# The MLP's down products: banks of shared products summed in DRAM, and two pairs of K tiles as seven products

## The chip, the cores and the metric

The kernel runs on one core of one Trainium2 chip. The metric is the device time in microseconds of one execution; lower is better. Every time below is of the same program and inputs.

## The reference

Two layers of a decoder trunk on 256 tokens of width 2048: an attention mixer (a different one in each layer), an MLP, and a gated per-layer embedding. The part that matters here is the MLP, once in each layer:

```python
hn = rmsnorm(h, mlp_norm_g[i])
h = h + jnp.square(jax.nn.relu(hn @ mlp_w1[i])) @ mlp_w2[i]     # 2048 -> 8192 -> 2048
```

All values are float32.

## The kernel before

**Precision.** TensorE works on `fp32r` values. Each operand is split into a high part and the rest (`whi`, `wlo` for weights), and a product of two tiles is three matmuls of 128x128 by 128x512 (`terms`): high by high, low by high, high by low. So the third matmul of a product is the first that reads `wlo`.

**The stream of weights.** All weights come in one long list of parts. `Program.run` walks it: for the part at position `at` it issues loads up to seven parts ahead (SyncE's queue, five `raw` buffers), the high cast up to four ahead (ScalarE, L249, six `whi` buffers), the low subtraction up to three ahead (VectorE, L257, five `wlo` buffers), then lets the helpers that are under way (generators, one step for each part) issue their next instructions, then issues the part's matmuls. All instructions of an engine run in the order in which they were issued; there is no scheduler behind that. A helper's `yield` thus means "after one more part". An operation that waits holds up all that is queued behind it on its engine.

**Seven products in place of eight.** A plain part multiplies two K tiles by both halves of the tokens: four products, 12 matmuls. Two parts (two output columns of 512) make eight products. `pair_major` makes the eight of a *mixed* pair of K tiles from seven (Strassen's scheme in Winograd's form). A mixed pair c takes four items: `a` (two products, 6 matmuls), `b` (one, 3 matmuls), `t` and `u` (two each). The weights of `t` and `u` are not loaded but made by VectorE: `make_t` (L537) from a and b, `make_u` (L542, L543) from a, b and t, in place in b's `raw` buffer. The input forms come as tile `hf` (in the downs) or `xf` (in the ups). The products end in the two pairs of PSUM banks `c_banks` (tile `at`) and in four shared banks `P1`, `R6`, `Q5`, `Q7` (tile `mm`), which `seven_sums` (L807 to L812: one ScalarE copy, four VectorE operations) turns into the parts that are added to the two outputs' banks.

**The MLP.** The 8192 hidden columns are four blocks b of 2048, each of four quarters q of 512. `ups` and `up_mixed` make a block's hidden values: a bank's result goes through ReLU with the norm factor (L828), a square (L765), a transposition on VectorE (L706), a bounce through DRAM on POOL's DMA queue (L203 out, four loads L207 in), and is split into tile `h` (cast L774, subtraction L776). The number of steps between the landing and the cast is in `REST`, by block and quarter. For one quarter `up` goes on and makes the forms `hf` of a mixed pair: four small subtractions (L784 to L787), a cast (L791), a subtraction (L793).

`down_mixed(b, q)` multiplies a block's hidden values by W2 for two output quarters q and q+1; one pair of eight, `MIXED_DOWN = 1`, is mixed. It ends with the bank added to the sums (L892) and `keep_sum`, which stores the first block's result to a DRAM tile `y[q]` and adds the later ones to it with an accumulating transfer (L849, POOL). In the last block the sums are fetched, added, turned and added to x. Quarters 2 and 3 of the last block are plain `downs`.

The order of a layer's MLP is `ups(0,0)` and `ups(0,1)`, `up_mixed(0,2)`, then for each block `down_mixed(b,0)`, `up_mixed(b+1,0)`, `down_mixed(b,2)`, `up_mixed(b+1,2)`, and at the end `down_mixed(3,0)` and the two plain downs. A down is named (b,q) below. Rows of [P, 2, 512] for all these come from `row_tile`, four buffers.

Of the kernel before, what the change touches and what calls it, by code (L numbers as in the profile page):

```python
# [28 lines left out]
NFB = 4  # L29
# [5 lines left out]
DMA_AHEAD = 7  # L35
SPLIT_AHEAD = 3
RAW_BUFS, HI_BUFS, LO_BUFS = 5, 6, 5
MIXED_DOWN = 1
MIXED = (2, 3, 5, 6)
REST = ((6, 8, 2, 3), (4, 4, 2, 3))  # L40

G_ATTN, G_MLP, G_PLE, G_KV, G_FIN = 0, 2, 4, 6, 7

# [6 lines left out]
def f32(ap):  # L50
    return ap.bitcast(F32)
# [116 lines left out]
def kernel(ctx: ExitStack, tc: tile.TileContext, a: dict, out: bass.AP):  # L168
    nc = tc.nc
# [525 lines left out]
    def turned(src, new, eng=nc.sync):  # L695

        z = new("z")  # L700
        z5 = z.rearrange("p (b i j r) -> p j i b r", b=4, i=4, j=2)
        if isinstance(src, (list, tuple)):
            for j in range(2):
                nc.vector.transpose(z5[:, j], src[j].rearrange("p (i b s) -> p i b s", b=4, s=32))
        else:
            nc.vector.transpose(z5, src.rearrange("p j (i b s) -> p j i b s", b=4, s=32))  # L706
        yield
        w = new("w").rearrange("p (a n) -> p a n", a=4)
        g = bounce(z, "dU", w, eng)
        next(g)  # L710
        yield
        yield
        next(g, None)
        yield
        yield
        return w
# [18 lines left out]
    def mlp(layer, xg, norm, to, norm2, opening):  # L735
# [4 lines left out]


        y = [dpool.tile([P, D // 2], F32, tag=f"y{q}", name=f"y{q}", bufs=1) for q in range(4)]
        hid = [[None] * 16 for _ in range(NFB)]
        forms = [None] * (KT // 2)
        sums_so_far = {}
        turned_forms = [[None] * (KT // 2) for _ in range(NFB)]
# [4 lines left out]
        def row():  # L751
            return row_tile()
# [9 lines left out]
        def up(b, q, t, late=0):  # L762
            rest = REST[b > 0][q]

            nc.scalar.activation(t, t, AF.Square)  # L765
            for _ in range(2 + late):
                yield
            w = yield from turned(t, second if b == 0 and q == 1 else other if q % 2 else new, nc.gpsimd)
            for _ in range(rest):
                yield  # L770
            w4 = w.rearrange("p a (i j r) -> p a (i j) r", j=2, r=32)
            h = cur["z"].tile([P, 2, 4, T], F32R, tag="h", name="h", bufs=4)
            h5 = h.rearrange("p c i (j a r) -> p c a (i j) r", j=2, r=32)
            nc.scalar.copy(h5[:, 0], w4)  # L774
            yield
            nc.vector.tensor_sub(h5[:, 1], w4, f32(h5[:, 0]))  # L776
            for i in range(4):
                hid[b][4 * q + i] = (h[:, 0, i], h[:, 1, i])
            if q != MIXED_DOWN // 2:
                return  # L780

            n = MIXED_DOWN % 2 * 4
            a11, a21, a12, a22 = (w4[:, :, n + i] for i in range(4))
            nc.vector.tensor_sub(a22, a21, a22)  # L784
            nc.vector.tensor_sub(a21, a11, a21)
            nc.vector.tensor_sub(a11, a11, a22)
            nc.vector.tensor_sub(a12, a12, a11)  # L787
            yield
            f = cur["z"].tile([P, 2, 2 * T], F32R, tag="hf", name="hf", bufs=1)
            f5 = f.rearrange("p c (i a r) -> p c a i r", i=4, r=32)  # L790
            nc.scalar.copy(f5[:, 0], w4[:, :, n:n + 4])  # L791
            yield
            nc.vector.tensor_sub(f5[:, 1], w4[:, :, n:n + 4], f32(f5[:, 0]))  # L793
            turned_forms[b][MIXED_DOWN] = f

        def up_plain(b, q, ps0, ps1, mm):

# [46 lines left out]
            sums_so_far[q] = row()  # L844
            nc.gpsimd.dma_start(flat(sums_so_far[q]), y[q])

        def keep_sum(b, q, t):

            nc.gpsimd.dma_start(y[q], flat(t), **({"accum_op": ALU.add} if b else {}))  # L849

        def down(b, q, ps0, ps1, mm):
            t = row() if b < NFB - 1 else sums_so_far[q]
            for j, ps in enumerate((ps0, ps1)):
                if b < NFB - 1:
                    nc.scalar.copy(t[:, j], ps)
                else:
                    nc.vector.tensor_add(t[:, j], ps, t[:, j])
            yield
            if b < NFB - 1:
                keep_sum(b, q, t)  # L860
                return
            w = yield from turned(t, second if q == 1 else new)
            add_turned(q, w)
            yield
            yield from in_pairs(normed, q)
# [10 lines left out]
        def all_forms(these):  # L876
            for c in these:
                yield from x_forms(2 * c, G_MLP + layer, forms)
                yield
        taken_late(lambda: ups(0, 0, {4: [lambda: norm.factor(rows=True)]}), lambda: ups(0, 1), opening,  # L880
                   [lambda: all_forms(MIXED[:3])])
        def down_mixed(b, q):
            ts = []

            def sums(aux):
                yield from seven_sums(aux, ts)

            def done(i, ps):
                while not ts:
                    yield  # L890
                t = ts[i]
                nc.vector.tensor_add(t, ps, t)  # L892
                yield
                if b < NFB - 1:
                    keep_sum(b, q + i, t)
                    return
# [6 lines left out]
                yield from in_pairs(normed, q + i)  # L903

            m = MIXED_DOWN
            p = [c for c in range(KT // 2) if c != m]
            order = [(0, c) for c in p[:3]]
            order += [(m,)] + [(1, c) for c in p[:3]] if b else [(1, c) for c in p[:3]] + [(m,)]
            for n in (3, 5):
                order += [(i, c) for i in range(2) for c in p[n:n + 2]]  # L910
            pair_major(lambda i, c: a["w2"][layer * 128 + (b * 4 + q + i) * 8 + c], order, hid[b], turned_forms[b],
                       sums, done, {13: [lambda: all_forms(MIXED[3:])]} if (b, q) == (0, 0) else None, (3, 1, 0, 2))

        up_mixed(0, 2)
        for b in range(NFB):
# [13 lines left out]
    def flat(t):  # L929
        return t.rearrange("p j c -> p (j c)")  # L930
# [968 lines left out]
def _layout(i):  # L1899
    a = dict(_tables())  # L1900
# [12 lines left out]
    a["w_oA"] = _quads(i["a_w_out"][0])  # L1913
    a["w1"] = np.concatenate([_mixed(_quads(i["mlp_w1"][l]), range(2, 16, 2), mixed) for l in range(2)])
    a["w2"] = np.concatenate([_mixed(np.concatenate([_quads(i["mlp_w2"][l, b * D:(b + 1) * D]) for b in range(NFB)]),
                                     range(0, 14, 2), lambda b, q: (MIXED_DOWN,)) for l in range(2)])
# [35 lines left out]
```

## Time and profile before

| | us |
|---|---|
| median of 3 runs | 2421.25 (2420.17 to 2422.47) |
| profiled execution, its own time | 2421.02 |
| span of its profile | 2419.1 |

| engine | busy us | share |
|---|---|---|
| TensorE | 2409.0 | 100% |
| VectorE | 1988.5 | 82% |
| ScalarE | 1420.2 | 59% |
| GpSimd | 122.0 | 5% |

Matmuls are pipelined, and their records overlap: a matmul of 128x512 has 389 ns, but one starts every 227 ns. "PE" is TensorE, "PEld" its weight loads, "DVE" VectorE, "ACT" ScalarE, "POOL" GpSimd, "SP" SyncE; a name such as L257 is a line of the kernel. In a row of a timeline stand the start, the time, the engine, line and operation, output and inputs, and in brackets the idle time before it and what ended that. Where a row ends in x3, three neighbours of one kind are merged.

### The profile page before, as it was taken

To read this page: it belongs to the slowest core of one execution; us is meant where nothing else is said; L and a number is where in the kernel's file an instruction comes from. 1 tells how busy PE (TensorE), PEld (TensorE's weight loads), DVE (VectorE), ACT (ScalarE), POOL (GpSimd) and SP (SyncE) were. 2 spreads that over 40 slices of the span, in tenths; PEclk is the share of its full clock that TensorE was granted. 3 is DMA by queue.
4 is the path that set the end of the run, shared out by engine and by line. 5 is a ranking of instruction groups with operands and counts; after the bars stand their busy time and mean duration, and the time that the engine had idled before them with its cause. 6 is when DMAs were issued, how large, how long until landed. Compare 5 with 4: busy or idle time off the path is not lost.

```text
span 2419.1 us, 33339 instructions
## 1 busy us (share of the span) xinstructions
PE 2409.0 (100%) x11643; PEld 2029.3 (84%) x11643; DVE 1988.5 (82%) x2944; ACT 1420.2 (59%) x2069; POOL 122.0 (5%) x214
## 2 busy tenths in 40 slices
PE   9999999999999999999999999999999999999998
PEld 8888888888888888888888889988888888888887
DVE  7867687688898898896777989867899898889776
ACT  6544444566555655564564788756655565556456
POOL 0000000000001000100000000000100100100000
PEclk9999999999999999999999999999999999999999
DMA  8667666777778777879786854477867877777974
GB/s 284 200 220 213 199 206 196 220 222 247 231 244 242 255 211 241 244 253 283 251 245 204 262 173 121 129 235 210 251 231 234 246 254 220 242 252 224 297 240 148
DMA packets 167271, 549.05 MB, mean 227 GB/s; under 512 B 20096, under 2 KB 35904, under 8 KB 167104
## 3 DMA queue, kind: packets, MB, share of 16 engines
q1 hardware_dynamic: 150672, 494.73, 63.7%
q0 software_dynamic: 15856, 51.41, 8.5%
q8 instruction: 91, 1.49, 0.3%
q10 hardware_dynamic: 576, 0.79, 0.1%
q14 instruction: 76, 0.62, 0.1%
HBM read 500.20 MB, written 46.66 MB: 226 GB/s over the span
## 4 chain that ended last, share of the span: by engine, by line
PE 98%; DMA 1%; DVE 0%; ACT 0%; issue 0%; ACTq 0%; DVEq 0%
PE at L499 40%; PE at L595 14%; PE mm L595 13%; PE mm L390 11%; PE mm L499 7%; PE mm L392 6%; PE at L390 1%; DMA raw<-in_w 1%; PE at L392 1%; PE at L1774 1%; PE mm L1798 0%; PE mm L1537 0%; PE mm L1538 0%; PE mm L1004 0%; PE mm L1006 0%; PE mm L1005 0%
## 5 line engine op out<-in xcount | busy, mean ns | idle before, releaser
L257 DVE TENSOR_TENSOR wlo<-raw,whi 128x1024 fp32r<-128x1024 f32 (+1 forms) x943 | 1090.6, 1176 | 247.3 <-ACT whi L249 63.9
L249 ACT CAST whi<-raw 128x1024 fp32r<-128x1024 f32 (+1 forms) x943 | 932.8, 1017 | 471.9 <-PE mm L595 101.8
L499 PE MATMUL at<-whi,h 128*128 128x512 f32 x1624 | 500.6, 389 | 0.4 <-DVE h L776 0.4
L390 PE MATMUL mm<-xa,whi 128*128 128x512 f32 x1104 | 372.4, 396 | 0.0
L499 PEld LDWEIGHTS at<-whi,h 128*128 128x128 f32 x1624 | 304.9, 188 | 64.6 <-DVE h L776 1.3
L499 PE MATMUL at<-whi,xa 128*128 128x512 f32 x1144 | 352.3, 389 | 0.0
L499 PE MATMUL at<-wlo,h 128*128 128x512 f32 x812 | 315.9, 389 | 0.0
L392 PE MATMUL mm<-xa,wlo 128*128 128x256 f32 x1104 | 274.2, 278 | 0.0
L499 PEld LDWEIGHTS at<-whi,xa 128*128 128x128 f32 x1144 | 214.7, 188 | 44.6
L499 PE MATMUL at<-wlo,xa 128*128 128x512 f32 x572 | 222.5, 389 | 0.0
L392 PEld LDWEIGHTS mm<-xa,wlo 128*128 128x128 f32 x1104 | 207.4, 188 | 17.6
L390 PEld LDWEIGHTS mm<-xa,whi 128*128 128x128 f32 x1104 | 193.5, 188 | 31.0 <-issue 0.4
L595 PE MATMUL at<-whi,xa 128*128 128x512 f32 x672 | 208.4, 392 | 0.0
L595 PE MATMUL mm<-whi,xa 128*128 128x512 f32 x656 | 202.7, 390 | 0.0
L499 PEld LDWEIGHTS at<-wlo,h 128*128 128x128 f32 x812 | 152.4, 188 | 31.5
L249 ACT CAST whi<-ts 128x1024 fp32r<-128x1024 f32 x68 | 71.5, 1051 | 156.8 <-DVE ts L537 106.9
L595 PEld LDWEIGHTS at<-whi,xa 128*128 128x128 f32 x672 | 125.2, 189 | 26.0 <-issue 0.6
L595 PEld LDWEIGHTS mm<-whi,xa 128*128 128x128 f32 x656 | 122.5, 188 | 25.0
L595 PE MATMUL at<-wlo,xa 128*128 128x512 f32 x336 | 130.8, 390 | 0.0
L595 PE MATMUL mm<-wlo,xa 128*128 128x512 f32 x328 | 127.7, 389 | 0.0
L499 PEld LDWEIGHTS at<-wlo,xa 128*128 128x128 f32 x572 | 107.4, 188 | 22.3
L499 PE MATMUL mm<-whi,xf 128*128 128x512 f32 x324 | 99.8, 389 | 0.0
(433 smaller groups left out, 3222.2 us busy)
## 6 DMA issues: line engine op xcount, KB each, us to landing
raw<-in_w SPq DMA_DIRECT2D x512, 512.0 KB, 4.8
raw<-in_w_qk SPq DMA_DIRECT2D x96, 512.0 KB, 4.1
raw<-in_w_gate SPq DMA_DIRECT2D x64, 512.0 KB, 4.5
raw<-in_w_kv SPq DMA_DIRECT2D x48, 512.0 KB, 4.4
raw<-in_w_v SPq DMA_DIRECT2D x47, 512.0 KB, 4.5
y<-y POOLq DMA_DIRECT2D x32, 512.0 KB, 5.5
raw<-in_w_q SPq DMA_DIRECT2D x32, 512.0 KB, 4.2
raw<-in_w_oB SPq DMA_DIRECT2D x32, 512.0 KB, 4.2
```

The source lines that it names most:

```text
L249: nc.scalar.copy(hi[:, c], t[:, c])
L257: nc.vector.tensor_sub(lo[:, c], t[:, c], f32(hi)[:, c])
L390: nc.tensor.matmul(ps, hi[:, col:col + P], rhs, start=first, stop=False)
L392: nc.tensor.matmul(ps[:, :T], lo[:, col:col + P], rhs[:, :T], start=False, stop=last)
L499: nc.tensor.matmul(ps, x_, w_, start=b not in touched, stop=end and last[b] == n and i == 2)
L595: nc.tensor.matmul(st[j], *parts[j][i], start=k == i == 0, stop=k == kt - 1 and i == 2)
L1774: nc.tensor.transpose(tr[:, i * P:(i + 1) * P], src, ident)
```

## The change

1. **Two mixed pairs in each `down_mixed`**: `MIXED_DOWN = (1, 0)`. Both come from quarter 0 of the block's hidden values, so `up` makes both `hf` tiles there (two buffers in place of one), and W2 is laid out accordingly.
2. **The order of items.** From block 1 on: two plain items for output quarter q, the first mixed pair, two plain items for q+1, the second mixed pair, then eight plain items. In block 0: four plain items, both mixed pairs one after the other, then eight plain items. Before, there were three plain items, the pair, three plain items and eight more (in block 0: six, the pair, eight).
3. **Sums of the shared banks.** In blocks 0 to 2 the four shared banks are copied by ScalarE into two rows, and these are stored or added to two more DRAM tiles for each pair of output quarters (`shared`). The outputs' own banks are copied by ScalarE and stored or added as they are. The two L892 additions and the four VectorE sums of these downs go.
4. **`flush`** makes the sums once for each pair of output quarters: it loads the two rows, makes the four VectorE operations after five steps, and adds the two results to `y`. For quarters 0 and 1 it starts after the first item of `down_mixed(2,2)`, for 2 and 3 after the first of `down_mixed(3,0)`. The last block's down (`down_last`) is summed as before.
5. `REST` for quarter 0 of blocks 1 to 3 is 8 in place of 4.

```diff
-MIXED_DOWN = 1
+MIXED_DOWN = (1, 0)
-REST = ((6, 8, 2, 3), (4, 4, 2, 3))
+REST = ((6, 8, 2, 3), (8, 4, 2, 3))
...
+        shared = {q: [dpool.tile([P, D // 2], F32, tag=f"s{q}{i}", name=f"s{q}{i}", bufs=1) for i in range(2)] for q in (0, 2)}
...
-            if q != MIXED_DOWN // 2:
+            if q:
                 return
-            n = MIXED_DOWN % 2 * 4
-            a11, a21, a12, a22 = (w4[:, :, n + i] for i in range(4))
-            ...
+            fs = {}
+            for c in MIXED_DOWN:
+                a11, a21, a12, a22 = (w4[:, :, 4 * c + i] for i in range(4))
+                nc.vector.tensor_sub(a22, a21, a22)
+                nc.vector.tensor_sub(a21, a11, a21)
+                nc.vector.tensor_sub(a11, a11, a22)
+                nc.vector.tensor_sub(a12, a12, a11)
+                fs[c] = cur["z"].tile([P, 2, 2 * T], F32R, tag="hf", name="hf", bufs=2)
+            ...
+            yield
+            for c in fs:
+                nc.scalar.copy(f5[c][:, 0], w4[:, :, 4 * c:4 * c + 4])
+            yield
+            for c in fs:
+                nc.vector.tensor_sub(f5[c][:, 1], w4[:, :, 4 * c:4 * c + 4], f32(f5[c][:, 0]))
...
-        def keep_sum(b, q, t):
-            nc.gpsimd.dma_start(y[q], flat(t), **({"accum_op": ALU.add} if b else {}))
+        def keep_sum(b, to, t):
+            nc.gpsimd.dma_start(to, flat(t), **({"accum_op": ALU.add} if b else {}))
...
+        def flush(q):
+            rows = r, o = row(), row()
+            for i in range(2):
+                nc.gpsimd.dma_start(flat(rows[i]), shared[q][i])
+            for _ in range(5):
+                yield
+            nc.vector.tensor_sub(r[:, 1], r[:, 1], r[:, 0])
+            nc.vector.tensor_add(o[:, 0], o[:, 0], r[:, 1])
+            nc.vector.tensor_sub(r[:, 1], o[:, 1], r[:, 1])
+            nc.vector.tensor_sub(o[:, 1], o[:, 0], o[:, 1])
+            yield
+            for i in range(2):
+                keep_sum(1, y[q + i], rows[i])
+
+        def down_kept(b, q):
+            def sums(aux):
+                for _ in range(4):
+                    yield
+                for i, names in enumerate((("P1", "R6"), ("Q5", "Q7"))):
+                    t = row()
+                    for j, n in enumerate(names):
+                        nc.scalar.copy(t[:, j], aux[n])
+                    yield
+                    keep_sum(b, shared[q][i], t)
+
+            def done(i, ps):
+                t = row()
+                nc.scalar.copy(t, ps)
+                yield
+                keep_sum(b, y[q + i], t)
+
+            return sums, done
...
+            sums, done = down_kept(b, q) if b < NFB - 1 else down_last(q)
             m = MIXED_DOWN
-            p = [c for c in range(KT // 2) if c != m]
-            order = [(0, c) for c in p[:3]]
-            order += [(m,)] + [(1, c) for c in p[:3]] if b else [(1, c) for c in p[:3]] + [(m,)]
-            for n in (3, 5):
+            p = [c for c in range(KT // 2) if c not in m]
+            if b:
+                order = [(0, p[0]), (0, p[1]), (m[0],), (1, p[0]), (1, p[1]), (m[1],)]
+            else:
+                order = [(i, c) for i in range(2) for c in p[:2]] + [(c,) for c in m]
+            for n in (2, 4):
                 order += [(i, c) for i in range(2) for c in p[n:n + 2]]
...
+                       {(0, 0): {13: [lambda: all_forms(MIXED[3:])]}, (NFB - 2, 2): {0: [lambda: flush(0)]},
+                        (NFB - 1, 0): {0: [lambda: flush(2)]}}.get((b, q)), (3, 1, 0, 2))
```

`down_last(q)` is the old `down_mixed`'s `sums` and `done` as they were for the last block.

More of the change, by code (lines that the diff above doesn't have):

```diff
@@ L778, in up @@
                 hid[b][4 * q + i] = (h[:, 0, i], h[:, 1, i])
-            if q != MIXED_DOWN // 2:
+            if q:
                 return
-            n = MIXED_DOWN % 2 * 4
-            a11, a21, a12, a22 = (w4[:, :, n + i] for i in range(4))
[L784 to L787, printed above, removed]
+            fs = {}
[6 more added lines that the diff above has]
+                fs[c] = cur["z"].tile([P, 2, 2 * T], F32R, tag="hf", name="hf", bufs=2)
+            f5 = {c: f.rearrange("p c (i a r) -> p c a i r", i=4, r=32) for c, f in fs.items()}
             yield
-            f = cur["z"].tile([P, 2, 2 * T], F32R, tag="hf", name="hf", bufs=1)
-            f5 = f.rearrange("p c (i a r) -> p c a i r", i=4, r=32)
-            nc.scalar.copy(f5[:, 0], w4[:, :, n:n + 4])
+            for c in fs:
+                nc.scalar.copy(f5[c][:, 0], w4[:, :, 4 * c:4 * c + 4])
             yield
-            nc.vector.tensor_sub(f5[:, 1], w4[:, :, n:n + 4], f32(f5[:, 0]))
-            turned_forms[b][MIXED_DOWN] = f
+            for c in fs:
+                nc.vector.tensor_sub(f5[c][:, 1], w4[:, :, 4 * c:4 * c + 4], f32(f5[c][:, 0]))
+                turned_forms[b][c] = fs[c]
         def up_plain(b, q, ps0, ps1, mm):
@@ L859, in down @@
             if b < NFB - 1:
-                keep_sum(b, q, t)
+                keep_sum(b, y[q], t)
                 return
@@ L881, in mlp, with down_last @@
                    [lambda: all_forms(MIXED[:3])])
-        def down_mixed(b, q):
+        def flush(q):
[27 more added lines that the diff above has]
+            return sums, done
+        def down_last(q):
             ts = []
@@ L893, in done @@
                 yield
-                if b < NFB - 1:
-                    keep_sum(b, q + i, t)
-                    return
                 nc.gpsimd.dma_start(flat(t), y[q + i], accum_op=ALU.add)
@@ L903, in done, with down_mixed @@
                 yield from in_pairs(normed, q + i)
+            return sums, done
+        def down_mixed(b, q):
+            sums, done = down_kept(b, q) if b < NFB - 1 else down_last(q)
             m = MIXED_DOWN
-            p = [c for c in range(KT // 2) if c != m]
-            order = [(0, c) for c in p[:3]]
-            order += [(m,)] + [(1, c) for c in p[:3]] if b else [(1, c) for c in p[:3]] + [(m,)]
-            for n in (3, 5):
+            p = [c for c in range(KT // 2) if c not in m]
[4 more added lines that the diff above has]
+            for n in (2, 4):
                 order += [(i, c) for i in range(2) for c in p[n:n + 2]]
-            pair_major(lambda i, c: a["w2"][layer * 128 + (b * 4 + q + i) * 8 + c], order, hid[b], turned_forms[b],
-                       sums, done, {13: [lambda: all_forms(MIXED[3:])]} if (b, q) == (0, 0) else None, (3, 1, 0, 2))
+            pair_major(lambda i, c: a["w2"][layer * 128 + (b * 4 + q + i) * 8 + c], order, hid[b], turned_forms[b], sums, done,
+                       {(0, 0): {13: [lambda: all_forms(MIXED[3:])]}, (NFB - 2, 2): {0: [lambda: flush(0)]},
+                        (NFB - 1, 0): {0: [lambda: flush(2)]}}.get((b, q)), (3, 1, 0, 2))
         up_mixed(0, 2)
@@ L1915, in _layout @@
     a["w2"] = np.concatenate([_mixed(np.concatenate([_quads(i["mlp_w2"][l, b * D:(b + 1) * D]) for b in range(NFB)]),
-                                     range(0, 14, 2), lambda b, q: (MIXED_DOWN,)) for l in range(2)])
+                                     range(0, 14, 2), lambda b, q: MIXED_DOWN) for l in range(2)])
     a["w_gate"] = np.concatenate([_quads(i["ple_w_gate"][l]) for l in range(2)])
```

## Prediction

> **What bounds the kernel now.** I read the page first: busy times and the chain that ended last.
>
> ```profile
> span 2419.1 us, 33339 instructions
> PE 2409.0 (100%) x11643; PEld 2029.3 (84%) x11643; DVE 1988.5 (82%) x2944; ACT 1420.2 (59%) x2069; POOL 122.0 (5%) x214
> PE 98%; DMA 1%; DVE 0%; ACT 0%; issue 0%; ACTq 0%; DVEq 0%
> ```
>
> TensorE (PE) is the chain. The view of waits, for PE alone, has two rows for the whole span, and the chain view tells what one matmul costs (27.88 us / 123 = 0.2267 us):
>
> ```profile
> PE mm L1180 <- DVE ones L219: 1.1, 1, 1.1
> PE at L499 <- DVE h L776: 0.4, 2, 0.3
> ```
> ```profile
> 632.87 27.88 PE at L499 x123
> ```
>
> So each matmul removed is worth 0.2267 us, if PE goes on being fed. Who feeds it is read by stage: the two MLP `ups` of block 0 (second half), then a `down_mixed` and an `up_mixed` of the steady part (length, then PE, PEld, DVE, ACT, POOL busy, granted clock, DMA share, GB/s):
>
> ```profile
> 515.00:557.00 42.00, 42.00 (x187) 34.77 (x186) 41.25 (x59) 29.13 (x40) 5.49 (x10) 1.00 0.72 226
> 728.30:771.20 42.90, 42.90 (x190) 35.50 (x190) 35.47 (x36) 23.02 (x26) 6.42 (x11) 1.00 0.80 242
> 771.20:812.00 40.80, 40.80 (x181) 33.78 (x180) 37.27 (x39) 24.69 (x28) 0.87 (x1) 1.00 0.76 235
> ```
>
> VectorE (DVE) is busy 41.25 of 42.00 us in the first, 83 and 91% in the others. It makes every `wlo`, and PE never waits for it: the kernel is balanced on the edge, and DVE is what the change loads.
>
> **The change, part by part.** Prices, from the views by tile and by line (ns min/median/max):
>
> ```profile
> L499 PE MATMUL mm<-wlo,hf x42: 389/389/389, 579.0 to 2233.8; 128*128 128x512 f32 x42
> L537 DVE TENSOR_TENSOR ts<-raw x68: 1180/1217/1221, 515.5 to 2225.3; 128x1024 f32<-128x1024 f32 x68
> L543 DVE TENSOR_TENSOR raw<-raw x68: 691/692/694, 519.3 to 2227.7; 128x512 f32<-128x512 f32 x68
> L809 DVE TENSOR_TENSOR y<-mm,y x28: 680/683/686, 554.7 to 2239.0; 128x512 f32<-128x512 f32 x28
> L892 DVE TENSOR_TENSOR y<-at,y x28: 1210/1225/1225, 598.9 to 2264.8; 128x1024 f32<-128x1024 f32 x28
> L807 ACT COPY y<-mm x28: 572/577/584, 552.2 to 2237.6; 128x512 f32<-128x512 f32 x28
> L849 POOL DMA_DIRECT2D y<-y x24: 554/859/929, 600.6 to 2182.7; - x24
> L845 POOL DMA_DIRECT2D y<-y x4: 874/892/908, 1102.4 to 2262.3; - x4
> DMA to landing us min/median/max: 9.3/10.1/11.0
> ```
>
> *PE.* 42 matmuls of three products a pair: 14 mixed pairs now. A second pair in each of the 14 `down_mixed` saves one product, 3 matmuls: 42 x 0.2267 = **9.5 us**. All on the path.
>
> *DVE in a down (b<3).* Added, per pair: `make_t` 1.22, `make_u` 2 x 0.69, and one and a half more `wlo` (1.8): +4.4. Removed: the four sums (4 x 0.69) and two bank adds (2 x 1.22): -5.2. About even, but moved: the added work comes early in the down, the removed work came late and at the next up's start. So DVE enters each up earlier by up to 2 x 1.22 = 2.4 us (the "lead").
>
> *ACT.* The copies of R6, Q5, Q7 (3 x 0.58), two banks (some 1.1 each, twice 0.58) and 1.5 casts (1.0 each by the row of ACT under B): +5.5 us per down on 23.0 of 42.9 busy. Hidden: they stand at items 16 to the next up's first, after the casts that PE needs next; a copy blocks the casts queued behind it while it waits for its bank, and those are four items (over 5 us) ahead.
>
> *POOL and DMA.* Per layer 12 more stores to the shared banks, 4 loads and 4 accumulating stores. POOL is busy 6.4 of 42.9 us; nobody waits for the stores. With the DMA share at 0.80 and 0.76 I cost the 20 transfers at nothing: cover is the five `raw` buffers. If it is gone, a load lands late and PE stops for that time; bounds 0 and, at 0.5 us per down, 7 us. I take 0, as PE waits for no load in any row.
>
> *REST 4 to 8* moves h of quarter 0 behind the last `m` item that reads the same buffer; cost nothing, nobody needs h before the block's end. It also takes one 1.2 us subtraction out of the early part of the second down of a block (used below).
>
> *Place A: hf for a second pair in block 0, in the up that is 98% DVE.* DVE, then PE (the third matmul of an item is the first to read its `wlo`):
>
> ```profile
> 541.05 1.22 DVE L776 TENSOR_TENSOR h<-w,h 128x1024 fp32r<-128x1024 f32 x1
> ...
> 543.49 0.69 DVE L542 TENSOR_TENSOR raw<-ts,raw 128x512 f32<-128x512 f32 x1
> ...
> 546.10 1.22 DVE L257 TENSOR_TENSOR wlo<-raw,whi 128x1024 fp32r<-128x1024 f32 x1
> 547.24 0.68 DVE L793 TENSOR_TENSOR hf<-w,hf 128x512 fp32r<-128x512 f32 x1
> 547.84 2.35 DVE L257 TENSOR_TENSOR wlo<-raw,whi 128x1024 fp32r<-128x1024 f32 x2
> ```
> ```profile
> 549.76 0.39 PE L499 MATMUL at<-wlo,xa 128*128 128x512 f32 x1
> ```
>
> The first `wlo` of the last row is ready at 549.0, PE wants it at 549.76: margin 0.75. Four more small subtractions (the four of now stand between h's end, 542.27, and 543.49: 1.2) and one more hf (0.6) put it 1.8 later: PE stops **1.05 us** (bounds 0 and 1.8), and DVE goes on 1.8 later than now.
>
> *Place B: block 0's first down, both mixed pairs together.* The down starts on PE at 560.18. DVE, then ACT:
>
> ```profile
> 560.18 0.62 PE L499 MATMUL at<-whi,h 128*128 128x512 f32 x2
> ```
> ```profile
> 565.42 1.21 DVE L826 TENSOR_TENSOR y<-at,y 128x1024 f32<-128x1024 f32 x1
> 566.55 1.21 DVE L257 TENSOR_TENSOR wlo<-raw,whi 128x1024 fp32r<-128x1024 f32 x1
> 570.06 2.36 DVE L257 TENSOR_TENSOR wlo<-raw,whi 128x1024 fp32r<-128x1024 f32 x2 [2.30 <-ACT whi L249]
> 572.34 1.24 DVE L706 STREAM_TRANSPOSE z<-y 128x1024 f32<-128x1024 f32 x1
> ```
> ```profile
> 569.00 2.50 ACT L249 CAST whi<-raw 128x1024 fp32r<-128x1024 f32 x3
> ```
>
> Now the mixed pair is items 6 to 9. After, items 4 to 11 are a,b,t,u,a,b,t,u. The bank add at 565.42 is late by 5.2 us against PE's start. It goes to 567.2 (A). From there DVE's order is: add, wlo a, make_t, wait for the cast of b (ACT's casts start 0.2 after its square, 570.8; wlo b at 571.45), wlo b, make_u, wlo t, transpose, wlo u, wlo a, make_t, wlo b, make_u, wlo t, h, wlo u. At pitches of 1.14 (1024 wide), 0.6, 1.33 (make_u) the last ends at 584.5. PE, starting at 561.2, has 84 matmuls ahead of that item (four plain items of 12; a, b, t, u of 6, 3, 6, 6; a, b, t), 19.04 us, and wants the `wlo` two matmuls later: 580.7. It stops **3.8 us** in all (first 1.8 of them at item 2, whose PSUM bank is freed by the add, at 568.4 instead of 566.7). Bounds: 3.0 without A's delay, 5 if a cast slips too. The old 0.4 us wait for h goes, as PE comes later.
>
> Second down of block 0: the lead (up to 2.4) and the missing h subtraction (1.1) take 3.5 off; what could be left, 0.3, I take as none.
>
> *Place C: flush, in the steady downs (2,2) and (3,0).*
>
> ```profile
> 1053.09 1.23 DVE L257 TENSOR_TENSOR wlo<-raw,whi 128x1024 fp32r<-128x1024 f32 x1 [0.32 <-ACT whi L249]
> ...
> 1061.59 1.23 DVE L257 TENSOR_TENSOR wlo<-raw,whi 128x1024 fp32r<-128x1024 f32 x1 [2.36 <-ACT whi L249]
> ...
> 1065.00 1.21 DVE L826 TENSOR_TENSOR y<-at,y 128x1024 f32<-128x1024 f32 x1
> ```
> ```profile
> 1062.47 0.61 PE L499 MATMUL at<-whi,h 128*128 128x512 f32 x2
> ```
>
> Same walk for (3,0), order q,q,a,b,t,u,q,q,a,b,t,u: from 1061.59 on wlo a, transpose, make_t, wlo b, add, make_u, wlo t, a 1.0 us wait for the cast of u, wlo u, wlo, transpose, wlo, wlo a, make_t, wlo b, make_u, wlo t, h, wlo u ends at 1082.5, 20.05 after PE's start; PE wants it at 19.49, as in B. With the lead that is no stop. The lead is at most 1.5 here: the `wlo` at 1053.09 takes the buffer of the up's item 19, which PE leaves at 1051.6 (180 matmuls, 40.8 us, lie between the up's start and 1062.47, and item 19 ends after 132 of them). The flush adds four serial DVE operations (2.65, as the four sums) just ahead of the second make_t: 22.7 - 1.5 - 19.49 = **1.7 us** stop in (3,0); in (2,2), which has no h subtraction there, the t item ahead of it decides (wanted after 78 matmuls and two: 18.13), 20.4 - 1.5 - 18.13 = **0.8**. Its two loads, issued by POOL behind the bounce store, take 10.1 to land, as the same kind does in the row above; they are needed some 10 to 11 us after their issue, so just in time. Bounds per layer: 1.1 (full lead) and 5.3 (none); I take 2.5, the lead that the row allows. In (3,0) the old DVE sums stay.
>
> **Sum**, against the profiled run (2421.02; span 2419.1 and 1.9 around it; 0.23 under the median 2421.25): -9.5 - 0.4 + 2 x (1.05 + 3.8 + 2.5) = +4.8. From the median: **2426.1 us**, +0.2%, which is about what a measurement can tell from no change.
>
> **Rivals.**
> *Fed all the way* (faster): no PE wait exists now although DVE is at 98%, so my walks may be pessimistic by the few us that decide; it needs DVE to run 4 us earlier at B. For: ACT takes 5.2 us per down off DVE. Against: in B no earlier down gives a lead, and DVE's own list alone is 3 us too long. 2421.25 - 9.9 = 2411.4; from there each place adds its price.
> *No lead at the flush* (slower): rows that land late, or a lead eaten by a late `raw`; C costs 5.3 per layer, 2421.25 + 4.8 + 5.6 = 2431.7. It decides above 1 us of lost lead. For: 10.1 us landing is just in time. Against: two bank adds do go.
> *Not what it says*: the shared banks' transfers delay loads, 7 us of the saving lost beside half the stalls: 2421.25 - 9.9 + 7.4 + 7 = about 2425.8.
> *DVE held by POOL's issues.* An accumulating issue now lies over a DVE operation:
>
> ```profile
> 850.92 0.92 POOL L849 DMA_DIRECT2D y<-y  x1 [21.40 <-issue]
> ```
> ```profile
> 850.29 1.22 DVE L537 TENSOR_TENSOR ts<-raw 128x1024 f32<-128x1024 f32 x1
> ```
>
> If issues held DVE, two loads of 0.89 at each of four flushes would stop PE 7.1 us more, 2433.2. The row speaks against it: 1.22 is this operation's usual time. [...]
>
> **How the numbers follow.** Forecast 0.48 (own range 2421 to 2431, about half of it beyond +0.2%), fed all the way 0.26, no lead 0.14, transfers 0.09, held 0.03. Faster 0.25, same 0.36, slower 0.39. The range has to take in most of the faster case and the no-lead one: 2412.5 to 2433.
>
> **What would show it.** PE: 42 matmuls fewer. PE's waits: for `wlo` near 549 and, in the first down of each layer, 3 to 4 us between 567 and 585 in the first layer; 1 to 2 us in (2,2) and (3,0), with the flush's DVE operations just ahead; none in (1,0), (1,2), (2,0). Wrong would be: no waits at B (the walk fails), or waits for `raw` or h spread over all downs (transfers).

## The result and the profile after

The changed kernel takes 2450.97 us (median of 4 runs, 2448.77 to 2454.65) against 2421.43 for the kernel before on the same chip: a ratio of 1.0124, 95% interval 1.0106 to 1.0141. It is slower by 1.2%, where +0.2% was forecast; the time lies 18 us above the upper end of the range. The profiled execution took 2454.65 us (span 2452.9).

The page of after: the span, the busy times, and the chain that ended last.

```profile
span 2452.9 us, 33573 instructions
PE 2419.4 (99%) x11601; PEld 2021.4 (82%) x11601; DVE 2013.6 (82%) x2998; ACT 1485.1 (61%) x2165; POOL 151.7 (6%) x254
PE 84%; DVE 6%; issue 4%; DMA 3%; ACT 2%; POOL 0%; SPq 0%; DVEq 0%; ACTq 0%; POOLq 0%
```

The 42 matmuls are gone (x11643 to x11601). The chain, 98% TensorE before, now runs through VectorE, ScalarE and DMA for 11% of the span. The four rows in which TensorE waits longest (us in total, times, longest):

```profile
PE mm L499 <- DVE wlo L257: 13.7, 20, 1.2
PE at L499 <- DVE wlo L257: 3.9, 7, 0.6
PE at L499 <- DVE y L829: 3.5, 4, 1.5
PE mm L295 <- DVE acc L286: 1.7, 2, 1.3
```

These rows hold 22.8 us of waits, where two rows with 1.5 us were all in before. They hold less than is lost: a wait counts from the end of a matmul's record of 389 ns, though the next matmul could start after 227, and matmuls at half the clock (the last section) are no wait. To see all of it, and where, I measure each stage from its first matmul to the next stage's first and take off its matmuls at 0.2267 us each; what is left is *lost*. Six stages by the view of windows (busy times, granted clock, DMA share, GB/s): the up (2,2), downs (2,0) and (2,2) with the up (3,0) between, the up (3,2), the first half of the end.

```profile
858.52:900.17 41.65, 41.51 (x182) 33.55 (x180) 37.09 (x39) 24.38 (x28) 0.84 (x1) 1.00 0.84 264
900.17:945.26 45.09, 43.38 (x187) 34.52 (x186) 37.19 (x36) 29.44 (x34) 8.19 (x13) 1.00 0.87 259
945.26:986.06 40.80, 40.80 (x181) 33.78 (x180) 36.03 (x37) 25.04 (x28) 0.84 (x1) 1.00 0.78 241
986.06:1031.59 45.53, 43.38 (x187) 34.67 (x186) 39.83 (x48) 27.14 (x32) 11.04 (x17) 1.00 0.85 256
1031.59:1076.16 44.57, 43.27 (x181) 34.71 (x180) 37.29 (x40) 25.88 (x30) 0.87 (x1) 0.96 0.81 254
1076.16:1121.00 44.84, 42.62 (x177) 33.47 (x176) 40.29 (x41) 25.04 (x28) 8.46 (x14) 0.96 0.87 275
```

A down of 186 matmuls should take 42.16 us: (2,0) loses 2.9 and (2,2) 3.4; an up of 40.80 loses 3.8 in the fifth row, where the granted clock is 0.96. All places, both layers added, for every kernel of this study (E is the end: (3,0) and the two plain downs; "other" the rest of the MLPs):

| kernel | place A, up (0,2) | place B, (0,0) | (2,0) | (2,2) and up (3,2) | E | other | sum | span |
|---|---|---|---|---|---|---|---|---|
| before | 0.0 | 1.1 | 0.0 | 0.0 | 0.0 | 0.0 | 1.0 | 2419.1 |
| after | 2.6 | 7.3 | 5.7 | 11.6 | 10.8 | 3.7 | 41.8 | 2452.9 |
| banks alone | 0.0 | 0.1 | 0.0 | 7.6 | 17.0 | 0.0 | 24.7 | 2442.5 |
| pairs alone | 2.6 | 7.3 | 3.0 | 4.2 | 3.3 | 13.6 | 34.0 | 2442.9 |
| fewer stores | 2.6 | 7.3 | 1.8 | 10.6 | 7.0 | 2.1 | 31.4 | 2440.5 |
| plain stores | 2.6 | 7.4 | 1.1 | 5.2 | 6.9 | 2.0 | 25.1 | 2434.2 |
| no flush | 2.6 | 7.4 | 4.9 | 1.0 | 16.4 | 2.6 | 34.8 | 2449.4 |
| banks, no flush | 0.0 | 0.9 | 0.0 | 0.0 | 3.8 | 0.0 | 4.6 | 2427.7 |
| no flush, block 0 one pair | 0.0 | 0.2 | 5.6 | 0.0 | 13.0 | 3.0 | 21.9 | 2436.8 |
| flush's sums on GpSimd | 2.6 | 7.4 | 5.2 | 13.4 | 16.5 | 4.6 | 49.6 | 2459.2 |
| flush without stores | 2.6 | 7.3 | 5.2 | 5.6 | 11.0 | 1.9 | 33.8 | 2443.2 |
| flush without sums | 2.6 | 7.4 | 5.6 | 4.3 | 10.1 | 3.9 | 33.8 | 2443.8 |
| no fold at the end | 2.6 | 7.3 | 5.0 | 0.5 | 6.0 | 2.1 | 23.6 | 2436.4 |
| second half plain | 2.6 | 7.4 | 1.3 | 0.3 | 9.8 | 1.7 | 23.2 | 2438.9 |
| first half plain | 2.6 | 7.4 | 4.4 | 0.6 | 11.2 | 2.0 | 28.1 | 2441.4 |
| all away | 0.0 | 1.2 | 1.6 | 0.0 | 5.6 | 1.5 | 10.0 | 2428.7 |

After loses 40.8 us more than before in the MLPs and saves 9.5: +31.3. Another 2.5 lie outside them (0.4 ahead of the first layer's up (0,2), 1.6 between the MLPs, 0.5 behind the second). That is the 33.8 by which the spans differ.

### The profile page after: what moved, and what is told of

Its sections match the earlier page's. It is cut to its first block, busy times and chain, and to the rows that moved or that the text cites. A ratio compares the mean times of both kernels' runs of the same rounds, so it can differ in the third digit from the quotient of the medians.

```text
span 2452.9 us, 33573 instructions
## 1 busy us (share of the span) xinstructions
PE 2419.4 (99%) x11601; PEld 2021.4 (82%) x11601; DVE 2013.6 (82%) x2998; ACT 1485.1 (61%) x2165; POOL 151.7 (6%) x254
## 3 DMA queue, kind: packets, MB, share of 16 engines
q1 hardware_dynamic: 150672, 494.73, 62.5%
q0 software_dynamic: 21616, 72.38, 11.5%
q8 instruction: 91, 1.49, 0.3%
## 4 chain that ended last, share of the span: by engine, by line
PE 84%; DVE 6%; issue 4%; DMA 3%; ACT 2%; POOL 0%; SPq 0%; DVEq 0%; ACTq 0%; POOLq 0%
PE at L499 29%; PE at L595 13%; PE mm L595 12%; PE mm L390 11%; PE mm L499 7%; PE mm L392 6%; DVE wlo L257 3%; DMA raw<-in_w 1%; PE at L390 1%; ACT whi L249 1%; DVE ts L537 1%; PE at L392 1%; DMA w<-dU 1%; PE at L1816 1%; DVE z L706 0%
## 5 line engine op out<-in xcount | busy, mean ns | idle before, releaser
L257 DVE TENSOR_TENSOR wlo<-raw,whi 128x1024 fp32r<-128x1024 f32 (+1 forms) x957 | 1098.4, 1170 | 259.9 <-ACT whi L249 91.7
L499 PE MATMUL at<-whi,h 128*128 128x512 f32 x1456 | 450.1, 390 | 3.0 <-DVE y L829 3.0
L499 PEld LDWEIGHTS at<-whi,h 128*128 128x128 f32 x1456 | 274.2, 189 | 60.8 <-issue 3.9
L499 PE MATMUL at<-wlo,h 128*128 128x512 f32 x728 | 284.3, 390 | 2.7 <-DVE wlo L257 2.7
L249 ACT CAST whi<-ts 128x1024 fp32r<-128x1024 f32 x82 | 86.4, 1053 | 170.3 <-DVE ts L537 144.7
L499 PEld LDWEIGHTS at<-wlo,h 128*128 128x128 f32 x728 | 137.1, 188 | 33.5 <-DVE wlo L257 4.8
L595 PEld LDWEIGHTS mm<-whi,xa 128*128 128x128 f32 x656 | 122.5, 188 | 25.1
L537 DVE TENSOR_TENSOR ts<-raw 128x1024 f32<-128x1024 f32 x82 | 99.6, 1215 | 5.8 <-DMA raw<-in_w 5.8
```

The costliest lines, as they stand in the source:

```text
L249: nc.scalar.copy(hi[:, c], t[:, c])
L257: nc.vector.tensor_sub(lo[:, c], t[:, c], f32(hi)[:, c])
L499: nc.tensor.matmul(ps, x_, w_, start=b not in touched, stop=end and last[b] == n and i == 2)
L537: nc.vector.tensor_add(halves(t), halves(a), b[:, None, :512].to_broadcast([P, 2, 512]))
L595: nc.tensor.matmul(st[j], *parts[j][i], start=k == i == 0, stop=k == kt - 1 and i == 2)
```

## The experiments

**The parts alone, and the stores.** The first theory (T1): the added accumulating stores delay weight loads. Its rival (T2): VectorE's added list of work.

*Banks alone* keeps the shared banks, the transfers and the flush, with one pair as before.

```diff
-MIXED_DOWN = (1, 0)
+MIXED_DOWN = (1,)
```

> The first part of the change alone: the shared banks, the 20 added transfers a layer and the flush are there, but only pair 1 of each down is mixed, in the order of the kernel before; so none of the 42 matmuls is saved. Theory T1 (the added accumulating stores delay weight loads, VectorE loses its lead in the ups and is late in the next down): the transfers are all there, TensorE still stops in D(2,0), D(2,2) and D(3,0), without the stops of the second pair in block 0 (5 us a layer), and nothing is saved: 2440 to 2452 us. Theory T2 (the second pair's VectorE work is what makes VectorE late, the transfers cost nothing): VectorE does less than in the kernel before, in every down, so only the flush's 2.5 us a layer may be left: 2419 to 2427 us.

Measured: 2444.9 us, ratio 1.0093 (1.0078 to 1.0108). T1's number, for another reason: it loses nothing in (1,0), (1,2), (2,0), with 24 stores into the shared banks running, and everything at the flush and behind it. In (3,0), VectorE and then POOL's queue:

```profile
1085.87 0.68 DVE L812 TENSOR_TENSOR y<-mm,y 128x512 f32<-128x512 f32 x1
1096.09 0.69 DVE L813 TENSOR_TENSOR y<-mm,y 128x512 f32<-128x512 f32 x1 [9.54 <-DMA y<-y]
```
```profile
1083.64 2.18 POOL L207 DMA_DIRECT2D y<-dU  x4 [6.39 <-ACT y L810]
1085.81 1.85 POOL L852 DMA_DIRECT2D y<-y  x2
```

The last down's sums take two of the four row buffers, and the second still belongs to the flush. Its sums end at 1081.4, but its stores are queued on POOL behind loads that wait 6.4 us for ScalarE (its copy at L810), and then take some 9 us to land. VectorE stands still for 9.5 us with all its `wlo` behind it, and TensorE waits 6.3.

*Pairs alone* keeps both pairs and the new order; each down makes its own sums, without banks, added transfers or flush.

```diff
-            sums, done = down_kept(b, q) if b < NFB - 1 else down_last(q)
+            sums, done = down_last(b, q)
...
+                if b < NFB - 1:
+                    keep_sum(b, y[q + i], t)
+                    return
```

> The second part of the change alone: pairs 1 and 0 of the downs as seven products, in the new order, but each down makes its own sums on VectorE as the kernel before does: no shared banks, no added transfer, no flush. T1 (the transfers are the cause): 9.5 us fewer of matmuls, some 5 us a layer of stops in block 0 (places A and B of the prediction), none in blocks 2 and 3: 2417 to 2427 us. T2 (VectorE's added work is the cause): VectorE carries the second pair's operations and also the sums of every down that the change took off it, so it is later than in the changed kernel everywhere: 2452 us or more.

Measured: 2446.11, ratio 1.0103 (1.0088 to 1.0118). T1's number falls; there is no added transfer in it, and it loses 34 us. T2's "2452 or more" is missed as well. The down (1,2) and the up behind it:

```profile
819.49:862.99 43.50, 42.46 (x188) 34.84 (x187) 39.70 (x47) 23.72 (x27) 6.01 (x11) 1.00 0.71 228
862.99:904.88 41.89, 41.09 (x181) 33.72 (x180) 39.12 (x43) 25.87 (x29) 1.30 (x2) 1.00 0.79 237
```

VectorE is busy 39.7 of 43.5 and 39.1 of 41.9 us, against 35 to 37 of 42.8 and 40.8 before, at a DMA share that is no higher. So a second pair with its sums in the same down is too much for VectorE by itself (1.3 us in the down, 1.1 in the up).

*Fewer stores* and *plain stores* take the transfers of the changed kernel apart.

```diff
-                    keep_sum(b, shared[q][i], t)
+                    if b == 0:
+                        keep_sum(b, shared[q][i], t)
```
```diff
-            nc.gpsimd.dma_start(to, flat(t), **({"accum_op": ALU.add} if b else {}))
+            nc.gpsimd.dma_start(to, flat(t), **{})
```

> The changed kernel with 8 of its 12 stores into the shared banks left out in each layer: blocks 1 and 2 keep only their y halves, so their shares of the shared sums are left out of the output. ScalarE's copies, the order, the flush and VectorE's work stay. T1: in D(1,0), D(2,0) and behind (1,2) and (2,0) the loads are no longer held up; the stops of D(1,0), D(2,0) and most of D(2,2) and D(3,0) go (0.7 + 2.9 + 2 + 3 us a layer): 2430 to 2440 us. T2: the list of work is the same, 2448 to 2453 us.

> The changed kernel with every store of a down's half made plain instead of accumulating: the same number of transfers, from the same tiles at the same places, but none reads and adds what lies in DRAM; the sums over the blocks are left out of the output. If T1 holds because an accumulating transfer takes longer on the DMA engines than a plain one, the loads beside them are held up less, and most of the stops in blocks 2 and 3 go: 2428 to 2442 us. If T1 holds by the number of transfers alone, or if T2 holds: 2446 to 2453 us.

Measured: 2439.56, ratio 1.0073 (1.0057 to 1.0090), and 2436.86, 1.0063 (1.0048 to 1.0078). Both in T1's range, 11 and 14 us under the changed kernel with VectorE's list unchanged. Plain stores move as many bytes; only the adding is gone. Queue 0 in after and in plain stores (packets, MB, share of 16 engines), and POOL's issues with their landing times:

```profile
q0 software_dynamic: 21616, 72.38, 11.5%
```
```profile
q0 software_dynamic: 21616, 72.38, 9.2%
```
```profile
L852 POOL DMA_DIRECT2D y<-y x32: 533/850/1277, 603.8 to 2275.2; - x32
...
DMA to landing us min/median/max: 5.5/9.1/13.3
```
```profile
L852 POOL DMA_DIRECT2D y<-y x32: 531/531/563, 603.7 to 2256.7; - x32
...
DMA to landing us min/median/max: 5.1/6.8/9.0
```

11.5% of 2452.9 less 9.2% of 2434.2 is 58 us of all sixteen engines, for 40 accumulating stores: 1.45 us each, on top of some 1.6 for a plain half (queue 1: 62.5% of 2452.9 us for 494.73 MB, 0.524 MB at a time). Adding in DRAM nearly doubles what a store takes here from the engines that bring the weights. (Of the 40 stores, 24 are new; 16 added in the kernel before, too.)

**The flush.** In after, (2,2), the up behind it and E hold 22.4 of the 41.8 us. *No flush* lets ScalarE copy the last block's four product banks into rows, adds the shared banks to them with accumulating loads and makes the four sums once from the rows; for the second half `fetch_shared` loads the shared banks where y2 and y3 were fetched, makes the sums after five steps, and adds y2 and y3 by accumulating loads ("fold at the end").

```diff
-                yield from seven_sums(aux, ts)
...
+                        nc.scalar.copy(rows[i][:, j], aux[n])
+                    yield
+                    nc.gpsimd.dma_start(flat(rows[i]), shared[q][i], accum_op=ALU.add)
...
+                sums_of(*rows)
...
-        prog.op(lambda: fetch(2))
-        prog.op(lambda: fetch(3))
+        prog.op(lambda: fetch_shared(2))
```

> The changed kernel with the flush gone: in (3,0) ScalarE copies the four product banks into two rows, accumulating loads add the shared banks to them, and the four sums are made once from these rows; for the second half the shared banks are loaded where y2 and y3 were fetched, summed, and y2 and y3 added by accumulating loads. Every result is still computed; four accumulating stores a layer and eight VectorE operations go, and nothing of it stands in front of a second mixed pair. Theory F (by now the first one: the flush itself, its VectorE work in (2,2) and (3,0), its rows and its late stores, is the largest part): most of the 22 us that TensorE loses in (2,2), the up behind it and (3,0) goes, places A and B and D(2,0) stay: 2428 to 2436 us. Theory T1 (the accumulating stores at the other borders delay loads and set VectorE back): the stops move little, 2443 to 2450 us.

> The shared banks alone (one mixed pair, the order of the kernel before, 24 stores into the shared banks in the two layers) with the same replacement of the flush: all results are computed. F: TensorE is fed as in the kernel before, 2419 to 2423 us, so some 22 us under the same kernel with the flush. T1: the stores still delay loads, 2430 us or more.

Measured: 2448.68, ratio 1.0111 (1.0094 to 1.0128); banks alone without flush 2427.48, ratio 1.0025 (1.0016 to 1.0035; its ten runs spread from 2421.6 to 2431.4). The first missed F's range by 12.7 us, the second by 4.5. The flush's place is indeed empty (11.6 to 1.0, and 7.6 to 0.0 with one pair), but E rose from 10.8 to 16.4, and 3.9 more went behind the MLPs. Forty us of the plain downs, in before and in no flush, and ScalarE there:

```profile
1105.00:1145.00 40.00, 40.00 (x179) 33.10 (x178) 30.33 (x39) 21.27 (x31) 3.44 (x7) 1.00 0.97 303
```
```profile
1110.00:1150.00 40.00, 36.92 (x163) 30.24 (x162) 25.03 (x27) 16.62 (x21) 6.08 (x10) 1.00 1.00 301
```
```profile
1142.86 1.05 ACT L249 CAST whi<-raw 128x1024 fp32r<-128x1024 f32 x1 [8.78 <-DMA raw<-in_w]
```

The DMA share was 0.97 there and is 1.00 now, and ScalarE stands 8.8 us for a weight; in before its longest such wait in the plain downs is 2.3. *No fold at the end* leaves out the two loads, the four sums behind them, and the adding in the two fetches:

```diff
-        prog.op(lambda: fetch_shared(2))
+        prog.op(lambda: fetch(2))
+        prog.op(lambda: fetch(3))
```

> The kernel without the flush, and the shared banks of the second half are never read back (their sums are left out of the output); y2 and y3 are fetched plainly, as in the kernel before. The plain downs at the end already have a DMA share of 0.97 there, 1.00 with the fold. If the two loads and the accumulating fetches are what holds up the weights there: the stop of 3.2 us near 1149 us, the clock's half window behind it and part of the waits after the MLP go, 6.7 and 4.9 us in the two layers and 2 us behind them: 2433 to 2439 us. If VectorE is late there for another reason: 2445 us or more.

Measured: 2436.9, ratio 1.0063 (1.0048 to 1.0078): as expected, 12 us back, 10.4 of them in E. The wait behind the second MLP stayed, though (`PE mm L295`, 2.1 us). The sums that went with the transfers are not the likely cause, as VectorE is busy 25.0 of the 40 us above; they were not left out alone.

Which part of the flush stops TensorE? *Flush without stores* and *flush without sums*:

```diff
-            for i in range(2):
-                keep_sum(1, y[q + i], rows[i])
```
```diff
-            nc.vector.tensor_sub(r[:, 1], r[:, 1], r[:, 0])
-            nc.vector.tensor_add(o[:, 0], o[:, 0], r[:, 1])
-            nc.vector.tensor_sub(r[:, 1], o[:, 1], r[:, 1])
-            nc.vector.tensor_sub(o[:, 1], o[:, 0], o[:, 1])
```

> The changed kernel with the flush's two loads and four VectorE sums in place, but without its two accumulating stores in each (so the shared sums never reach the output). If the sums alone stop TensorE: the 2.3 us at 1004 to 1007 us and their like in (3,0) and layer 2 stay, while the late loads behind them (ScalarE's 5.2 us wait at 1010 to 1015 us) and the 3.8 us in the up behind go: 2440 to 2446 us. If the stores matter nothing: 2449 to 2453 us.

> The changed kernel with the flush's loads and stores in place, but without VectorE's four sums between them (the products go into y unsummed). If there is no lead, the four operations, 2.9 us, are what stops TensorE 2.2 us in (2,2), and more in (3,0): these stops go, the late loads behind the stores stay: 2438 to 2445 us. If the lead of the prediction had been there, taking the sums away gains 0.8 and 1.7 us a layer at most: 2446 to 2449 us.

Measured: 2445.26, ratio 1.0100 (1.0085 to 1.0115), and 2444.8, 1.0094 (1.0077 to 1.0111). Both gains came as expected in sum: neither part is the cause alone. With the sums only, (2,2) loses 2.6 and 2.8 us and the up behind it almost nothing; with the stores only 1.8 and 1.1, and 0.7 in each up. Together they lose 11.6, against 5.6 and 4.3 alone; 3.0 of the 11.6 are matmuls at half the clock (below), which neither kernel has there. In E neither gains much (11.0 and 10.1, against 10.8): without the sums the stops 18 to 23 us into (3,0) are smaller, as expected, but others come 34 to 40 us into it. VectorE, POOL and ScalarE in (2,2) of after:

```profile
999.39 0.69 DVE L891 TENSOR_TENSOR y<-y 128x512 f32<-128x512 f32 x1
...
1001.56 0.69 DVE L894 TENSOR_TENSOR y<-y 128x512 f32<-128x512 f32 x1
1002.17 1.22 DVE L537 TENSOR_TENSOR ts<-raw 128x1024 f32<-128x1024 f32 x1
```
```profile
1007.93 1.87 POOL L852 DMA_DIRECT2D y<-y  x2
```
```profile
1015.45 1.05 ACT L249 CAST whi<-raw 128x1024 fp32r<-128x1024 f32 x1 [5.17 <-DMA raw<-in_w]
```

The sums stand 2.8 us ahead of the second `make_t`; six us later the two stores start, and ScalarE stands 5.2 us for the next weight. Without the stores this wait was to go; it is still 3.3. But *no fold at the end*, which has no flush at all, has 3.3 there, too, and before at most 2.0: what the rest of this wait is made of stays open.

*The flush's sums on GpSimd* was to move them off VectorE.

```diff
-            nc.vector.tensor_sub(r[:, 1], r[:, 1], r[:, 0])
+            nc.gpsimd.tensor_sub(r[:, 1], r[:, 1], r[:, 0])
...
```

> The changed kernel with the flush's four sums computed by GpSimd instead of VectorE, in the same place; loads and stores as they were. If VectorE's four operations in front of the second mixed pair are what stops TensorE in (2,2) and (3,0) (2.3 us each and the clock's half windows behind them): the stops at 1004 to 1007 and 1095 to 1102 us and their like in layer 2 go, 2438 to 2444 us. If it is the flush's rows and transfers: 2448 us or more, the more so if GpSimd's sums delay its own transfers.

Measured: 2460.84, ratio 1.0167 (1.0152 to 1.0182), the slowest of all. By its number it is in the second range, but what the rows show is VectorE, not rows or transfers. GpSimd and VectorE in (2,2):

```profile
1003.51 1.77 DVE L257 TENSOR_TENSOR wlo<-raw,whi 128x512 fp32r<-128x512 f32 x1
1005.21 1.77 DVE L542 TENSOR_TENSOR raw<-ts,raw 128x512 f32<-128x512 f32 x1
1007.01 0.69 DVE L543 TENSOR_TENSOR raw<-raw 128x512 f32<-128x512 f32 x1
```
```profile
1002.59 2.15 POOL L893 TENSOR_TENSOR y<-y 128x512 f32<-128x512 f32 x1
1004.81 1.62 POOL L894 TENSOR_TENSOR y<-y 128x512 f32<-128x512 f32 x1
```

While GpSimd computes, a VectorE operation of 0.69 us takes 1.77; with GpSimd's end it is 0.69 again. In (2,2) four operations of VectorE grow by 1.1 us each, 4.4 in all, more than the four of 0.69 that it was spared.

**Block 0, and which stores hurt (2,0).** *Block 0 one pair* is no flush with pair 1 alone in block 0, in the old order.

```diff
-MIXED_DOWN = (1, 0)
+MIXED_DOWN = ((1,), (1, 0), (1, 0), (1, 0))
```

> The kernel without the flush, and in block 0 only pair 1 as seven products, in the order of the kernel before; the second pair stays in blocks 1 to 3. It gives back 12 matmuls (2.7 us) and should take away places A (1.3 us a layer) and B (3.65 us a layer): 7.2 us under the kernel without the flush, if A and B are what the prediction said: 2420 to 2429 us. If the stops of A and B only move to the next downs (VectorE is late anyway): 2428 to 2437 us.

Measured: 2439.52, ratio 1.0077 (1.0062 to 1.0092), 9.2 under no flush, where 7.2 were expected; the absolute range was missed with its base. The up (0,2) and the down (0,0):

```profile
519.06:560.54 41.48, 41.48 (x185) 34.36 (x183) 40.36 (x56) 27.14 (x37) 5.50 (x10) 1.00 0.79 241
560.54:603.43 42.89, 42.89 (x190) 35.41 (x189) 34.63 (x38) 29.50 (x37) 7.12 (x13) 1.00 0.89 289
```

No stop of note is left in either (0.2 us in the two layers): A and B come with the second pair in block 0 and its order of items. They did not move to the next downs: (2,0) loses 5.6 against 4.9, the rest of the MLPs 3.0 against 2.6.

*Second half plain* takes the adding (and so the sums over the blocks) out of the stores of quarters 2 and 3 in the kernel without flush; *first half plain*, with `q != 0`, out of the others.

```diff
-            nc.gpsimd.dma_start(to, flat(t), **({"accum_op": ALU.add} if b else {}))
+            nc.gpsimd.dma_start(to, flat(t), **({"accum_op": ALU.add} if b and q != 2 else {}))
```

> The kernel without the flush, with plain instead of accumulating stores in the second half's downs (0,2), (1,2), (2,2) alone (their sums over the blocks are left out). T1, by now for the places D(2,0) and D(3,0) only: these stores run during the up that precedes a first-half down, delay its weights and set VectorE back; D(2,0) falls from 2.4 to about 0.5 us in each layer, D(3,0) likewise: 2440 to 2444 us. If the stores don't matter there: 2447 to 2450 us.

> The same kernel with the plain stores in the first half's downs (0,0), (1,0), (2,0) instead. By T1 they run in front of second-half downs, which have no subtraction of h early and stop nowhere: D(2,0) and D(3,0) stay at 2.4 us, 2446 to 2450 us. If any accumulating store sets VectorE back for good, both kinds give the same gain, some 3 to 4 us each: 2443 to 2446 us.

Measured: 2438.17, ratio 1.0067 (1.0052 to 1.0082), and 2444.19, 1.0093 (1.0077 to 1.0110). The down (2,0) of no flush, of second half plain and of first half plain:

```profile
899.09:943.68 44.59, 43.22 (x188) 34.53 (x186) 37.16 (x36) 28.73 (x33) 8.17 (x13) 1.00 0.84 256
```
```profile
898.59:941.37 42.78, 42.45 (x187) 34.83 (x186) 36.19 (x36) 27.49 (x31) 8.13 (x13) 1.00 0.85 262
```
```profile
898.74:943.66 44.92, 43.38 (x188) 34.53 (x186) 37.23 (x36) 29.12 (x34) 7.17 (x13) 1.00 0.85 271
```

44.59 falls to 42.78 only with the stores that run in the up before (2,0); the others leave it at 44.92 (in the second layer 2.4 us of loss fall to 0.7, and to 1.7). VectorE in the up before, in no flush:

```profile
865.43 1.23 DVE L537 TENSOR_TENSOR ts<-raw 128x1024 f32<-128x1024 f32 x1 [1.49 <-DMA raw<-in_w]
```

The stores to `y` start at 854.9 and 860.6, and `make_t` waits 1.49 us for a weight; with the second half plain it waits for none there. So at (2,0) T1 holds, and by place. In time both kernels gained more than T1 said (10.5 and 4.5 us; the end also improved, 16.4 to 9.8 and 11.2). The second number lies in the rival's range, but the gains are not the same: the first half's stores aren't free either, and how they act stays open.

*All away* combines: no flush, one pair in block 0, all stores plain, no fold.

> All suspected causes away at once: no flush, pair 1 alone in block 0, every store of a half plain, and the shared banks of the second half never read back (the sums over the blocks and that half's shared sums are left out of the output). 30 of the 42 matmuls stay saved, 6.8 us. If flush, places A and B, accumulation and the fold at the end are all of the loss, only the 0.5 us stops in blocks 1 to 3 are left (some 3 us): 2416 to 2420 us, under the kernel before. If something else in the list of work stops TensorE: 2424 us or more.

Measured: 2428.33, ratio 1.0024 (1.0013 to 1.0035): not the 2416 to 2420 expected. Up to (3,0) of the first layer it runs 1.4 us ahead of before (PE reaches it at 1061.1 instead of 1062.5). What is lost is 4.9 us in the second layer's E, and 3.4 and 3.9 behind the two MLPs, where this row stands (from 1170 to 1182 us the granted clock is 0.91, and 1.00 in before):

```profile
PE mm L295 <- DVE acc L286: 3.8, 2, 2.3
```

Why the norm's sums come late there stays open; of the end's transfers only the two accumulating loads in each (3,0) are not those of before. Its ten runs spread from 2421.0 to 2434.0.

## Why the prediction was wrong, step by step

- **A and B were right.** 2.6 us for 2 x 1.05 (in two stops a layer, where one was forecast), 7.3 for 2 x 3.8 (1.63 of the first at item 2, by the bank add; 1.8 was predicted). The walk along VectorE's order holds to a few tenths where nothing outside that order acts.
- **The step that failed first is the lead at place C.** It was priced at 2.5 us a layer with up to 1.5 us of lead; after loses 11.2 a layer at (2,2), up (3,2) and E. VectorE does get ahead in a down, but it gives the lead back in the first items of the up. VectorE in the up (3,0), in before and in after:

```profile
941.00 2.58 DVE L257 TENSOR_TENSOR wlo<-raw,whi 128x1024 fp32r<-128x1024 f32 x2 [0.42 <-issue]
```
```profile
945.53 1.22 DVE L257 TENSOR_TENSOR wlo<-raw,whi 128x1024 fp32r<-128x1024 f32 x1 [1.49 <-PE at L499]
948.24 2.58 DVE L257 TENSOR_TENSOR wlo<-raw,whi 128x1024 fp32r<-128x1024 f32 x2 [1.48 <-PE at L499]
```

  In after VectorE waits twice for TensorE, 1.49 and 1.48 us: L257 writes nothing but a `wlo` buffer, and TensorE is still reading it. The pair of the last row then starts 37.82 us ahead of the next down (986.06), in before 37.83 (978.83). The second of the pair waits 0.13 us for TensorE in after and 0.14 in before, and before has this wait in every up of blocks 1 to 3: there was no room for a lead in the kernel as it stood. From there to the border VectorE's list is the same in both. The `wlo` at the border, behind the 2.36 us of idle time that the prediction shows, comes 1.01 us ahead of (2,2) in after and 0.65 to 1.08 ahead of the downs (1,0) to (3,0) in before. I bounded the lead at the `wlo` of 1053.09, late in the up, where 1.5 us were left, and not at the up's first ones. With plain stores the place shows its price without a lead: 2.4 and 2.8 us in (2,2), 3.4 and 3.5 in (3,0), 12.1 in all. The walk gives 20.4 - 18.13 = 2.3 and 22.7 - 19.49 = 3.2; that is 5.5 a layer (0.8 with the full lead), where the prediction's bounds say 5.3 (and 1.1). So its rival "no lead at the flush" was right for that half, though what took the lead was neither late rows nor a late `raw`.
- **The 20 transfers at nothing** failed by more. Leaving out 8 of the 12 stores to the shared banks in each layer takes away 10.4 us of loss (41.8 to 31.4), and taking the adding out of all 40 accumulating stores 16.7 (41.8 to 25.1): 4.6 in (2,0), 10.3 in place C and E, 1.7 elsewhere. The bound of 7 us, 0.5 a down, was no bound: I took it from a mean DMA share of 0.80, and a late weight shows where the down that follows has no slack. "None in (2,0)" is wrong by 5.7 us. In the two kernels with one pair the same stores cost nothing at (2,0), and neither VectorE nor ScalarE waits for a weight early in the up before it: it takes the second pair as well. Why the weights are late only with it was not tested.
- **What the sum lacked.** The forecast holds 14.7 us of loss, and 41.8 came. Of the 27.1 between, 16.7 go with the adding, 7.1 are place C without a lead, and 3.1 are left with plain stores in (0,2), (1,0) and (2,0), which were put at none (the last 0.2 are A and B).
- **Half the clock.** Twenty-five matmuls of after stand at a pitch of 0.427 us, 5.0 us in all; plain stores have none in the MLP, so these are part of the 16.7. It was in no term.
- **The saving** of 9.5 us is real, but the first-half downs (1,0) and (2,0) lose 0.7 to 0.9 us each even in all away, as much as the 0.68 that a second pair saves in one. Only (1,2) and (2,2) take it for nothing there: 12 matmuls, 2.7 us, less than the 6.3 that the shared banks cost without flush and with one pair (2427.48 against 2421.18). None of the versions beats the kernel before.
- **Other rivals.** "Fed all the way" fell at A and B. "Shared banks' transfers" was right in kind, but its 7 us are less than half of the 16.7. "Held by POOL's issues" fell: beside an issue of a transfer VectorE's operations keep their time in before and in after (`make_t` takes 1.22 us at 850.29 in before, and 1.22 at 1029.32 in after, beside the issue of 1028.74 to 1029.59), and they grow only where GpSimd computes (1.77 in place of 0.69 us, above). The new order of items and `REST` came with the second pair in every kernel; neither was tested alone.

## What to carry to other kernels

A lead did not pass VectorE's waits that end on TensorE's own progress here (1.49 and 1.48 us): before counting on one, go through the feeder's waits from the start of the stage on, and look for the first one that TensorE ends, however short. A transfer that adds in DRAM took about twice the DMA time of a plain one here (some 1.6 + 1.45 us of all sixteen engines against 1.6); price it at the stage that follows it, and look for a stage near a DMA share of 1.0 before moving anything there (the plain downs went from 0.97 to 1.00 in no flush, and ScalarE stood 8.8 us for a weight). Work that waits to be done once still needs a place where the feeder has slack.

## What the runs showed of the hardware

A short stop cost TensorE more than itself here. The trace of after has four stretches of 3.41 us at a granted clock of 0.50 in the MLPs, each behind waits for a `wlo` of at most 1.2 us; the matmuls in the four cost 5.0 us more. The stretch ahead of the first one, that one, and the one behind it:

```profile
1050.55:1053.96 3.41, 2.11 (x8) 0.89 (x7) 3.32 (x6) 2.29 (x3) 0.00 (x0) 1.00 0.26 80
1053.96:1057.37 3.41, 3.41 (x9) 2.63 (x10) 3.41 (x4) 2.22 (x3) 0.00 (x0) 0.50 0.61 187
1057.37:1060.78 3.41, 3.41 (x17) 2.80 (x16) 3.38 (x5) 1.36 (x2) 0.00 (x0) 1.00 0.67 211
```

After 3.41 us in which TensorE was busy 2.11, the granted clock is 0.50 for the next 3.41 us, some eight matmuls start instead of fifteen, and then it is back. The first stretch takes 3.413 us by the edges of its clock, and the other three start 44.4, 1129.8 and 1218.6 us behind it, 13.0, 331.0 and 357.0 times 3.413: in this trace all four lie on one grid. TensorE was not idle for the whole step of the grid ahead of a half one: the four steps there are busy for 1.58 to 2.11 us of 3.41. Nor does such a share decide by itself; a step of the same grid that is busy for less (1.95, with a wait of 1.47 us), in the first layer's (0,0), 488.1 us or 143.0 steps ahead of the first half one, and the step behind it, at a granted clock of 1.00:

```profile
565.85:569.26 3.41, 1.95 (x9) 1.36 (x8) 3.41 (x4) 0.61 (x2) 0.56 (x1) 1.00 0.76 227
569.26:572.67 3.41, 3.41 (x16) 2.78 (x16) 2.67 (x4) 3.38 (x5) 0.00 (x0) 1.00 0.70 219
```

What else decides stays open.
